# 128-column matmuls of the expert stages: issued in one or two bursts per expert pair, instead of at eleven places among the 64-column ones

## The chip, the cores and the metric

One core of a Trainium2 chip runs the whole program in one launch. The metric is the device time of that launch in microseconds (us). TensorE does the matmuls, VectorE (DVE) and ScalarE (ACT) empty its result banks, GpSimd (POOL) helps in the attention stages, and the SyncE queue (SP) issues the loads of the weights.

## What is computed

Two layers over 256 latent and 256 context tokens of width 1024. Each has a token mixer (windowed attention, then differential attention) and then a mixture of 32 SwiGLU experts, of which each token uses two. The last layer computes the latent tokens alone. What matters here is the mixture:

```python
def run(args):                       # one expert's tokens
    xblk, e = args
    u = xblk @ w_up[e]               # (tokens, 1024) @ (1024, 1024)
    return (silu(u[:, :512]) * u[:, 512:]) @ w_down[e]
yb = lax.map(run, (xb, blk_expert)).reshape(NB * MOE_BLOCK, D)
return zeros((T, D)).at[stok].add(yb[dest] * sw[:, None])
```

The router's choice of two experts for each token, and its weight `sw`, come just before. An expert has 1024x1024 weights up and 512x1024 weights down, all float32.

## The kernel before, in words

The function `moe` runs once for each layer. T is the number of tokens, 512 in layer 0 and 256 in layer 1. It takes the 32 experts as 16 **pairs**. An expert has room for 64 tokens, so a pair fills 128 rows: the first expert's matmuls write partitions 0 to 63 of a result bank, the second's write 64 to 127. Such a matmul has a 64-column weight operand (the tokens) and streams 512 columns of an expert's weights. This is what "64-column" means; the profile prints it as 128\*64, and one float32 matmul is two records. All others of the stage have 128 columns (128\*128).

One pair goes through these steps on TensorE, in this order:

- `up` (line 1195), for k = 0 to 7: four 64-column matmuls (8 records), which is one **step**. After it two loaded weight slots come free.
- `combine` (line 1276), after each of the eight steps: two 128-column matmuls of T columns that spread 128 output features of the previous pair back over the tokens. VectorE's `gated_add` (line 506) then adds the bank to the residual stream, 256 columns at a time.
- `gate` (lines 1202 to 1204): ScalarE and VectorE form the SwiGLU product from the two result banks of `up`.
- `gather` for the next pair, all 128-column: the routing weights' product (line 1174, emptied by the copies of lines 1177 and 1179), the first half of the token gather (line 1142), the transpose of the selection matrix (line 1158), then `turned` (line 1227), which transposes the gate's product, and the second half of the gather (line 1142).
- `down` (line 1239), four steps of 64-column matmuls. After the second and the third step `spread_tokens` (line 1184) transposes one half of the next pair's tokens, four 128-column transposes each time; VectorE adds the shift (line 1186). These are what the next pair's `up` reads.
- `weigh` (lines 1266 and 1267): ScalarE and VectorE scale the result and split it into two parts, which the next pair's `combine` reads.

In the last pair (`final`) `combine` starts only after step k = 3 (`HOLD` is 3), and three of the eight are done between the last `up` and the transposes of `gate_last`. In pair 0 there is nothing to combine. Pair 5 (`IF_AT`) has a branch after its `up` steps, for the case that an expert has more than 64 tokens.

Four things set the order. TensorE's order is that of the code (`manual_schedule(engines=PE)`). VectorE's and ScalarE's is chosen by a scheduler. The weights are loaded by one queue on SyncE, 24 loads of 512 KB a pair, each as soon as the slot that it writes has been read by TensorE. And the result banks are used in turn: `bank("G")`, `bank("C")`, `bank("B")` each rotate over two banks, and a matmul that starts on a bank waits until the engine that empties it is done.

```python
for k in range(KT):
    up(st, u, k)
    ...
    if prev and k >= HOLD * final:
        combine(l, T, prev, k - HOLD * final)
```

## Time and profile before

| | |
|---|---|
| runs | 1627.4, 1627.59, 1629.95 us; median 1627.59 us |
| profiled execution | span 1629.6 us from its first to its last instruction; only the run of 1629.95 us is as long, so 0.35 us lie around the span |
| TensorE busy | 1542.0 us, 95% |
| VectorE busy | 710.0 us, 44% |
| ScalarE busy | 383.5 us, 24% |
| loads from memory | 485.67 MB, mean 298 GB/s |

The time splits into stages: the modulation and attention of layer 0 until about 300 us, the experts of layer 0 until about 857 us, the attention of layer 1 until about 1105 us, the experts of layer 1 until about 1620 us, and the end. "Busy" of TensorE is an interval from an instruction's start to an end that the profile models, so 95% does not say that no time is lost between matmuls; the starts of the rows do.

### The profile page before, as it was taken

To read this page: it belongs to the slowest core of one execution; us is meant where nothing else is said; L and a number is where in the kernel's file an instruction comes from. 1 tells how busy PE (TensorE), PEld (TensorE's weight loads), DVE (VectorE), ACT (ScalarE), POOL (GpSimd) and SP (SyncE) were. 2 spreads that over 40 slices of the span, in tenths; PEclk is the share of its full clock that TensorE was granted. 3 is DMA by queue.
4 is the path that set the end of the run, shared out by engine and by line. 5 is a ranking of instruction groups with operands and counts; after the bars stand their busy time and mean duration, and the time that the engine had idled before them with its cause. 6 is when DMAs were issued, how large, how long until landed. Compare 5 with 4: busy or idle time off the path is not lost. (4 is left out here: it accounts for less than half of the span.)

```text
span 1629.6 us, 20216 instructions
## 1 busy us (share of the span) xinstructions
PE 1542.0 (95%) x7407; PEld 775.9 (48%) x7407; DVE 710.0 (44%) x1617; ACT 383.5 (24%) x823; POOL 185.2 (11%) x147
## 2 busy tenths in 40 slices
PE   6998999799999999999997889899999999999997
PEld 4765567443334444334435678673333333333334
DVE  3338852433333433333348977862232223232323
ACT  4426652101000111001114245651001100110112
POOL 2314541000000000000005373100000000000000
PEclk9999999899999999999997999998999999999999
DMA  9776236799989989999962842487999999999960
GB/s 315 236 232 225 90 104 225 298 362 366 377 323 360 377 349 363 375 374 375 362 200 88 294 166 103 170 294 298 405 402 351 397 401 402 398 394 400 403 241 27
DMA packets 169695, 485.67 MB, mean 298 GB/s; under 512 B 20825, under 2 KB 41586, under 8 KB 169586
## 3 DMA queue, kind: packets, MB, share of 16 engines
q1 hardware_dynamic: 169088, 483.66, 78.3%
q8 instruction: 63, 1.03, 0.3%
q10 hardware_dynamic: 498, 0.60, 0.1%
q14 instruction: 46, 0.38, 0.1%
HBM read 483.16 MB, written 1.05 MB: 297 GB/s over the span
## 5 line engine op out<-in xcount | busy, mean ns | idle before, releaser
L1195 PE MATMUL ps<-slotf,row 128*64 128x512 f32 x2048 | 492.4, 604 | 1.6 <-DVE row L1186 1.6
L506 DVE SCALAR_TENSOR_TENSOR slotf<-ps,mod,slotf 128x256 f32<-128x256 f32 x408 | 184.2, 481 | 382.5 <-PE ps L1276 349.8
L1195 PEld LDWEIGHTS ps<-slotf,row 128*64 128x64 f32 x2048 | 128.7, 136 | 228.2 <-issue 186.4
L1239 PE MATMUL ps<-slotf,row 128*64 128x512 f32 x960 | 225.8, 602 | 0.0
L543 PE MATMUL ps<-slotr,slotr 128*128 128x512 f32 x768 | 192.4, 403 | 11.1 <-DVE slotf L1395 5.7
L1276 PEld LDWEIGHTS ps<-row,row 128*128 128x128 f32 x512 | 76.3, 188 | 197.9 <-issue 177.2
L543 PEld LDWEIGHTS ps<-slotr,slotr 128*128 128x128 f32 x768 | 144.5, 193 | 48.9 <-DVE slotf L1395 6.1
L1276 PE MATMUL ps<-row,row 128*128 128x512 f32 (+1 forms) x512 | 156.4, 389 | 3.4 <-DVE slotf L506 3.3
L1202 ACT ACTIVATE row<-ps 128x512 f32<-128x512 f32 x30 | 17.9, 597 | 523.8 <-PE ps L1195 481.5
L1239 PEld LDWEIGHTS ps<-slotf,row 128*64 128x64 f32 x960 | 60.8, 136 | 112.6 <-issue 111.5
L1186 DVE TENSOR_TENSOR row<-ps,mod 128x512 f32<-128x512 f32 x64 | 44.2, 691 | 152.3 <-PE ps L1184 152.3
L1266 ACT ACTIVATE row<-ps,ty 128x512 fp32r<-128x512 f32 x60 | 41.2, 687 | 273.2 <-PE ps L1239 272.9
L518 POOL TENSOR_TENSOR slotr<-slotf,slotr 128x1024 fp32r<-128x1024 f32 x32 | 80.1, 2516 | 91.2 <-ACT slotr L514 78.9
L478 POOL TENSOR_TENSOR row<-row,row 128x512 f32<-128x512 f32 (+1 forms) x13 | 15.0, 1156 | 614.2 <-PE ps L1276 558.1
L1142 PE MATMUL ps<-slotr,row 128*128 128x512 f32 x256 | 70.9, 421 | 0.0
L1142 PE MATMUL ps<-slotf,row 128*128 128x512 f32 x128 | 66.3, 642 | 2.2 <-DVE s L1028 0.9
L1267 DVE SCALAR_TENSOR_TENSOR row<-ps,ty,row 128x512 fp32r<-128x512 f32 x60 | 45.0, 751 | 35.4 <-ACT row L1266 32.2
L514 ACT ACTIVATE slotr<-slotf 128x1024 fp32r<-128x1024 f32 x44 | 45.9, 1055 | 51.0 <-DMA slotf<-in_diff_w_qkv 23.8
L1142 PEld LDWEIGHTS ps<-slotr,row 128*128 128x128 f32 x256 | 48.1, 198 | 12.6 <-ACT row L1152 2.7
L1184 PEld LDWEIGHTS ps<-ident,row 128*128 128x128 f32 x256 | 27.0, 141 | 51.4 <-issue 50.3
L1494 DVE SCALAR_TENSOR_TENSOR row<-slotf,keep,row 128x512 f32<-128x512 f32 x42 | 49.2, 1184 | 1.1
L1358 PE MATMUL ps<-slotr,slotr 128*128 128x512 f32 x192 | 47.6, 399 | 0.0
(311 smaller groups left out, 1547.5 us busy)
## 6 DMA issues: line engine op xcount, KB each, us to landing
slotf<-in_moe_w_up SPq DMA_DIRECT2D x512, 512.0 KB, 6.7
slotf<-in_moe_w_down SPq DMA_DIRECT2D x256, 512.0 KB, 7.5
slotf<-in_mod_w SPq DMA_DIRECT2D x96, 512.0 KB, 6.2
slotf<-in_diff_w_qkv SPq DMA_DIRECT2D x24, 512.0 KB, 4.4
slotf<-in_win_w_qkv SPq DMA_DIRECT2D x12, 512.0 KB, 5.2
slotf<-in_win_w_o SPq DMA_DIRECT2D x8, 512.0 KB, 4.2
slotf<-in_diff_w_o SPq DMA_DIRECT2D x8, 512.0 KB, 3.8
slotf<-in_x SPq DMA_DIRECT2D x2, 512.0 KB, 4.2
```

The source lines that it names most:

```text
L506: ve.scalar_tensor_tensor(xT[k][:, sl], ps[:, sl], g[:, k, r:r + 1], xT[k][:, sl], op0=OP.mult, op1=OP.add)
L514: se.activation(hv, v, AF.Copy)
L518: (eng or (ge if split_i[0] % 3 == 0 else ve)).tensor_tensor(lv, v, hv.bitcast(F32), op=OP.subtract)
L543: pe.matmul(ps[t], h[:, x, ts], w[y][:, kk, :], start=(k + kk == 0 and n == 0), stop=(k + kk == KT - 1 and n == 2))
L1142: pe.matmul(g, P[:, t, :] if len(tok[t]) > 1 else P[:, t, :].bitcast(F32), v[:, hs], start=(t == 0 and i == 0), stop=(t == nt - 1 and i == ...
L1186: ve.tensor_tensor(o.rearrange("p (k c) -> p k c", k=4), ps.rearrange("p (k c) -> p k c", k=4), mods[l][:, 3, 4 * h:4 * h + 4, 0:1].to_bro ...
L1195: pe.matmul(u[h][64 * s:64 * s + 64, :], st["xt"][k // 4][:, c0:c0 + 64], w[s][1][:, h * 512:(h + 1) * 512], start=(k == 0), stop=(k == KT ...
L1239: pe.matmul(y[h][64 * s:64 * s + 64, :], acT[:, c0:c0 + 64], w[s][1][:, h * 512:(h + 1) * 512], start=(k == 0), stop=(k == 3))
L1267: ve.scalar_tensor_tensor(yl, y[h], wsl, yh.bitcast(F32), op0=OP.mult, op1=OP.subtract)
L1276: pe.matmul(ps[:, :T], part[:, ks], st["PT"][:, :T], start=(i == 0), stop=(i == 1))
L1358: pe.matmul(ps, w[x][:, k % 4, ms], oT0[k][1][:, y, :], start=(k == 0 and i == 0), stop=(k == KT - 1 and i == 2))
L1494: ve.scalar_tensor_tensor(acc, w[:, kk, :], keep[:, k + kk:k + kk + 1], acc, op0=OP.mult, op1=OP.add)
```

## The change

The table `HOLD` goes. Each pair's 128-column work moves to one or two places:

- Layer 0 (T = 512): the first four `combine` steps stand together after k = 3, behind the transposes of the second half of the tokens; the other four stand after k = 7, directly before `gather`.
- Layer 1 (T = 256): all eight stand after k = 7. Two of them share one result bank.
- The banks of `combine` are now C, C, B, B in turn. Before they were C alone.
- `spread_tokens` leaves `down`. In layer 0 the first half is transposed at the end of `gather` and the second half at k = 3 of the next pair. In layer 1 both halves are transposed at the end of `gather`, and the routing weights' product moves behind the second half of the gather.
- In the last pair `gate_last` calls the remaining `combine` steps in place of three of them.

```diff
--- before.py
+++ after.py
@@ -45,7 +45,6 @@
 MODS = range(0, 24, 3)
 LATE = (0,) * 4 + (4,) * 4 + (3,) * 4 + (1,) * 4 + (0,) * 8
 IF_AT = 5
-HOLD = 3
 BIG = 1e30
 RSQRT = float(0x5F3759DF)
 
@@ -1052,6 +1051,8 @@
 
         np_ = NE // 2
         prev = st = None
+        early_ks = range(0, KT // 2) if T == 512 else ()
+        late_ks = range(len(early_ks), KT)
         for p in range(np_):
             u = [bank("A"), bank("A")]
 
@@ -1062,15 +1063,18 @@
                     up(st, u, k)
                     if p == 0 and k == 1:
                         st["half"]()
-                    if p == 0 and k == 2:
-                        spread_tokens(l, st, 1)
-                        gather_weights(st["P"], WR, p, st, 2)
-                    if prev and k >= HOLD * final:
-                        combine(l, T, prev, k - HOLD * final)
+                    if k == KT // 2 - 1:
+                        if len(st["xt"]) < 2:
+                            spread_tokens(l, st, 1)
+                        if p == 0:
+                            gather_weights(st["P"], WR, p, st, 2)
+                        if prev:
+                            combine(l, T, prev, early_ks)
 
             if p == IF_AT:
                 with tc.manual_schedule(engines=PE):
                     ups()
+                    combine(l, T, prev, late_ks)
                 hs_ = [Slot() for _ in range(KT // 2)]
                 stream.ahead(len(free) - 1)
                 most = nc.values_load(cmi[0:1, 0:1], min_val=0, max_val=T)
@@ -1083,12 +1087,14 @@
                     st = gather(l, nt, 0, key, WR, tok, unit, weights, ri=post.ri)
                 if p != IF_AT:
                     ups()
+                rest = partial(combine, l, T, prev, late_ks) if prev and p != IF_AT else lambda: None
                 if final:
-                    acT = gate_last(u, [partial(combine, l, T, prev, k) for k in range(KT - HOLD, KT)])
+                    acT = gate_last(u, rest)
                 else:
                     ac = gate(u)
+                    rest()
                     nxt = gather(l, nt, p + 1, key, WR, tok, unit, None, lambda: turned(ac))
-                    y = down(nxt["acT"], partial(spread_tokens, l, nxt))
+                    y = down(nxt["acT"])
                     prev = {"parts": weigh(y, st["w"][:, 0:1]), "PT": st["PT"]}
                     st = nxt
         with tc.manual_schedule(engines=PE):
@@ -1098,7 +1104,7 @@
 
             def finals(c):
                 for k in (2 * c, 2 * c + 1):
-                    combine(l, T, {"parts": {k // 4: parts[c]}, "PT": st["PT"]}, k, k % 2)
+                    combine(l, T, {"parts": {k // 4: parts[c]}, "PT": st["PT"]}, (k,), k % 2)
                     last.append(after(k))
                     if len(last) > 2:
                         last.pop(0)()
@@ -1131,8 +1137,8 @@
                 for t in range(nt):
                     pe.matmul(wps[:, 0:1], P[:, t, :].bitcast(F32), ri[:, t:t + 1], start=(t == 0), stop=(t == nt - 1))
                 ve.tensor_copy(st["w"][:, 1:2], wps[:, 0:1])
-        else:
-            gather_weights(P, WR, p, st, 2 if unit else 3)
+        elif not unit:
+            gather_weights(P, WR, p, st, 3)
 
         def half(h):
             hs = slice(h * 512, (h + 1) * 512)
@@ -1165,6 +1171,10 @@
             st["half"] = partial(half, 1)
         else:
             half(1)
+            if unit:
+                gather_weights(P, WR, p, st, 2)
+            for h in range(1 + unit):
+                spread_tokens(l, st, h)
         return st
 
     def gather_weights(P, WR, p, st, n):
@@ -1204,7 +1214,7 @@
         ve.scalar_tensor_tensor(ac, ac, 0.5, u[1], op0=OP.mult, op1=OP.mult)
         return ac
 
-    def gate_last(u, between):
+    def gate_last(u, rest):
         th, ac, acT = row("s"), row("s"), row("x")
         halves = [slice(h * 256, (h + 1) * 256) for h in range(2)]
         for hs in halves:
@@ -1212,8 +1222,7 @@
         for hs in halves:
             ve.scalar_tensor_tensor(ac[:, hs], th[:, hs], 1.0, u[0][:, hs], op0=OP.add, op1=OP.mult)
             ve.scalar_tensor_tensor(ac[:, hs], ac[:, hs], 0.5, u[1][:, hs], op0=OP.mult, op1=OP.mult)
-        for f in between:
-            f()
+        rest()
         for h, hs in enumerate(halves):
             ps = bank("G")
             for k in range(2):
@@ -1229,7 +1238,7 @@
         se.activation(acT, ps, AF.Copy)
         return acT
 
-    def down(acT, spread=None):
+    def down(acT):
         y = [bank("B"), bank("B")]
         for k in range(4):
             w = [stream.next() for _ in range(2)]
@@ -1240,8 +1249,6 @@
                               w[s][1][:, h * 512:(h + 1) * 512], start=(k == 0), stop=(k == 3))
             for s in range(2):
                 w[s][0].free()
-            if spread and k in (1, 2):
-                spread(k - 1)
         return y
 
     def down_last(acT, c, wsl):
@@ -1268,13 +1275,21 @@
             parts.append((yh, yl))
         return parts
 
-    def combine(l, T, st, k, place=None):
-        ps = bank("C")
-        place = k % 4 if place is None else place
-        ks = slice(place * 128, (place + 1) * 128)
-        for i, part in enumerate(st["parts"][k // 4]):
-            pe.matmul(ps[:, :T], part[:, ks], st["PT"][:, :T], start=(i == 0), stop=(i == 1))
-        gated_add(l, 1, k, ps, T)
+    def combine(l, T, st, ks, place=None):
+        per = 512 // T
+        adds = []
+        for n, k in enumerate(ks):
+            if n % per == 0:
+                ps = bank("CCBB"[n // per % 4])
+            c = k % 4 if place is None else place
+            out = ps[:, (n % per) * T:(n % per + 1) * T]
+            for i, part in enumerate(st["parts"][k // 4]):
+                pe.matmul(out, part[:, c * 128:(c + 1) * 128], st["PT"][:, :T], start=(i == 0), stop=(i == 1))
+            adds.append((k, out))
+            if (n + 1) % per == 0 or n + 1 == len(ks):
+                for kk, v in adds:
+                    gated_add(l, 1, kk, v, T)
+                adds = []
 
     def overflow(l, nt, key, W, ri, tok, hT):
         T = nt * 128
```

Three places of the order of instructions show what moved. In `order` rows, `x4` means four alike in a row, and ps is a result bank.

TensorE in layer 0, pair 9, around the `up` step k = 3 (ps_5189, ps_5190 or ps_5182, ps_5183 are the two banks of `up`). Before, one step, its `combine`, and the next step:

```order
L1195 MATMUL ps_5189<-slotf_79,row_5159 64x512
L1195 MATMUL ps_5189<-slotf_55,row_5159 64x512
L1195 MATMUL ps_5190<-slotf_79,row_5159 64x512
L1195 MATMUL ps_5190<-slotf_55,row_5159 64x512
L1276 MATMUL ps_5232<-row_4927,row_5180 128x512
L1276 MATMUL ps_5232<-row_4927,row_5181 128x512
L1195 MATMUL ps_5189<-slotf_57,row_5172 64x512
```

The same place now:

```order
L1205 MATMUL ps_5183<-slotf_55,row_5145 64x512
L1194 MATMUL ps_5210<-ident,row_5138 128x128 x4
L1287 MATMUL ps_5217<-row_4927,row_5173 128x512
L1287 MATMUL ps_5217<-row_4927,row_5174 128x512
L1287 MATMUL ps_5222<-row_4927,row_5173 128x512
L1287 MATMUL ps_5222<-row_4927,row_5174 128x512
L1287 MATMUL ps_5227<-row_4927,row_5173 128x512
L1287 MATMUL ps_5227<-row_4927,row_5174 128x512
L1287 MATMUL ps_5232<-row_4927,row_5173 128x512
L1287 MATMUL ps_5232<-row_4927,row_5174 128x512
L1205 MATMUL ps_5182<-slotf_57,row_5215 64x512
```

One spread (line 1194) and four `combine` steps (line 1287) now stand in one run; between the other steps of `up` nothing is left.

VectorE in layer 0, at the end of a pair's `up`, from the gate's first multiplication (lines 1203 and 1213) to the drain of the gather's second half (lines 1150 and 1156). Before:

```order
L1203 SCALAR_TENSOR_TENSOR row_4896<-row_4895,ps_4803 128x512
L506 SCALAR_TENSOR_TENSOR slotf_133<-ps_4890,mod_236,slotf_133 128x256 x2
L1204 SCALAR_TENSOR_TENSOR row_4896<-row_4896,ps_4804 128x512
L1177 COPY ty_4902<-ps_4903 64x1 x2
L1179 COPY ty_4902<-ps_4903 128x1
L1150 TENSOR_SCALAR row_4945<-ps_4936,ty_4902 128x512
```

Now:

```order
L1213 SCALAR_TENSOR_TENSOR row_4876<-row_4875,ps_4796 128x512
L505 SCALAR_TENSOR_TENSOR slotf_135<-ps_4880,mod_236,slotf_135 128x256
L1214 SCALAR_TENSOR_TENSOR row_4876<-row_4876,ps_4797 128x512
L505 SCALAR_TENSOR_TENSOR slotf_135<-ps_4880,mod_236,slotf_135 128x256
L505 SCALAR_TENSOR_TENSOR slotf_135<-ps_4885,mod_236,slotf_135 128x256 x2
L505 SCALAR_TENSOR_TENSOR slotf_133<-ps_4890,mod_236,slotf_133 128x256 x2
L505 SCALAR_TENSOR_TENSOR slotf_133<-ps_4895,mod_236,slotf_133 128x256 x2
L1187 COPY ty_4902<-ps_4903 64x1 x2
L1189 COPY ty_4902<-ps_4903 128x1
L1156 TENSOR_SCALAR row_4945<-ps_4936,ty_4902 128x512
```

Eight adds now stand ahead of the copies of the routing weights (lines 1187 and 1189), where two stood.

TensorE in layer 1, from the gather's transposes to the first step of `down`. Before:

```order
L1227 MATMUL ps_10244<-ident,row_10222 128x128 x4
L1142 MATMUL ps_10251<-slotf_79,row_10226 128x512
L1142 MATMUL ps_10251<-slotf_55,row_10226 128x512
L1239 MATMUL ps_10256<-slotf_91,row_10249 64x512
L1239 MATMUL ps_10256<-slotf_81,row_10249 64x512
```

Now:

```order
L1236 MATMUL ps_10207<-ident,row_10162 128x128 x4
L1148 MATMUL ps_10214<-slotf_79,row_10194 128x512
L1148 MATMUL ps_10214<-slotf_55,row_10194 128x512
L1184 MATMUL ps_10219<-WR_8357,row_10194 128x2 x2
L1194 MATMUL ps_10224<-ident,row_10200 128x128 x4
L1194 MATMUL ps_10231<-ident,row_10217 128x128 x4
L1248 MATMUL ps_10238<-slotf_91,row_10212 64x512
```

The routing weights' product and both spreads now stand between the second half of the gather (line 1148) and `down` (line 1248); all four use the two banks of tag G in turn, so the first spread's bank is the one that the gather's second half was written to.

## Rows read from the trace of the kernel before

**Rows 1.** The page: the span, the engines' busy time, and the granted TensorE clock in 40 slices (tenths of full speed).

```profile
span 1629.6 us, 20216 instructions
PE 1542.0 (95%) x7407; PEld 775.9 (48%) x7407; DVE 710.0 (44%) x1617; ACT 383.5 (24%) x823; POOL 185.2 (11%) x147
...
PEclk9999999899999999999997999998999999999999
```

**Rows 2.** The chain that ended last: shares of the span by engine, and by line.

```profile
PE 20%; ACT 0%; DVE 0%; issue 0%; DVEq 0%; ACTq 0%
PE ps L1195 9%; PE ps L1239 4%; PE ps L1142 2%; PE ps L1276 2%; PE ps L1184 1%; PE ps L1253 0%; ACT row L1148 0%; PE ps L1174 0%; PE ps L491 0%; PE ps L1721 0%; DVEq L1768 0%; DVE slotf L506 0%; DVE row L1213 0%; ACT row L1211 0%; DVE row L1214 0%
```

**Rows 3.** Sums over stretches: one pair of layer 0, one gather in layer 0, one pair of layer 1, twelve us inside that pair, and the gather behind the branch of layer 0. The columns are the stretch, its length, busy time of PE, PEld, DVE, ACT and POOL with their counts, the granted clock, the DMA engines' busy share, and GB/s.

```profile
650.30:684.60 34.30, 34.30 (x156) 13.99 (x154) 12.90 (x27) 3.66 (x7) 0.00 (x0) 1.00 0.95 371
...
669.80:676.20 6.40, 6.40 (x38) 5.08 (x36) 2.48 (x7) 1.66 (x3) 0.00 (x0) 1.00 1.03 410
...
1428.60:1460.20 31.60, 31.51 (x140) 11.67 (x138) 9.22 (x18) 3.29 (x7) 0.00 (x0) 1.00 1.02 400
...
1436.00:1448.00 12.00, 12.00 (x56) 4.53 (x53) 3.55 (x8) 0.60 (x1) 0.00 (x0) 1.00 1.03 410
...
495.70:500.60 4.90, 4.82 (x16) 4.04 (x17) 1.75 (x5) 0.51 (x1) 0.00 (x0) 0.55 1.03 405
```

**Rows 4.** TensorE's timeline in layer 0: `down` with its spreads, some `up` and `combine` steps, and the next gather. The columns are start, length, engine, line, and the number of records; in brackets the idle time before and what ended it.

```profile
641.90 3.65 PE L1239 MATMUL ps<-slotf,row 128*64 128x512 f32 x16
645.49 0.66 PE L1184 MATMUL ps<-ident,row 128*128 128x128 f32 x4
...
647.94 0.66 PE L1184 MATMUL ps<-ident,row 128*128 128x128 f32 x4
...
652.11 0.73 PE L1276 MATMUL ps<-row,row 128*128 128x512 f32 x2
...
654.64 0.73 PE L1276 MATMUL ps<-row,row 128*128 128x512 f32 x2
...
669.83 0.73 PE L1276 MATMUL ps<-row,row 128*128 128x512 f32 x2
670.39 0.95 PE L1174 MATMUL ps<-WR,row 128*128 128x3 f32 x8
671.20 2.09 PE L1142 MATMUL ps<-slotr,row 128*128 128x512 f32 x8
673.13 0.60 PE L1158 MATMUL ps<-ident,row 128*128 128x128 f32 x4
673.57 0.60 PE L1227 MATMUL ps<-ident,row 128*128 128x128 f32 x4
```

**Rows 5.** TensorE's timeline in the last two pairs of layer 1; the columns as in Rows 4.

```profile
1578.42 3.65 PE L1239 MATMUL ps<-slotf,row 128*64 128x512 f32 x16
...
1586.81 7.04 PE L1195 MATMUL ps<-slotf,row 128*64 128x512 f32 x32
1593.78 0.50 PE L1276 MATMUL ps<-row,row 128*128 128x256 f32 x2
...
1596.08 0.50 PE L1276 MATMUL ps<-row,row 128*128 128x256 f32 x2
```

**Rows 6.** TensorE's timeline in the attention of layer 0: a run of eight 128-column matmuls of 256 columns, which follows 64-column ones; the columns as in Rows 4.

```profile
143.33 1.21 PE L757 MATMUL ps<-slotr,slotr 128*128 128x256 f32 x8
144.38 1.03 PE L782 MATMUL ps<-ident,row 128*128 128x128 f32 x8
```

**Rows 7.** The timeline of all engines in layer 0, behind the last `up` step of a pair; the columns as in Rows 4.

```profile
669.74 0.69 DVE L1203 SCALAR_TENSOR_TENSOR row<-row,ps 128x512 f32<-128x512 f32 x1 [0.80 <-ACT row L1202]
...
670.59 0.88 DVE L506 SCALAR_TENSOR_TENSOR slotf<-ps,mod,slotf 128x256 f32<-128x256 f32 x2 [0.16 <-PE ps L1276]
...
671.38 0.68 DVE L1204 SCALAR_TENSOR_TENSOR row<-row,ps 128x512 f32<-128x512 f32 x1
...
672.31 0.16 DVE L1179 COPY ty<-ps 128x1 f32<-128x1 f32 x1
...
673.38 0.69 ACT L1152 ACTIVATE row<-ps,ty 128x512 f32<-128x512 f32 x1 [3.67 <-PE ps L1142]
...
674.12 2.12 PE L1142 MATMUL ps<-slotr,row 128*128 128x512 f32 x8
...
676.17 3.65 PE L1239 MATMUL ps<-slotf,row 128*64 128x512 f32 x16
```

**Rows 8.** The timeline of all engines in layer 1: the second half of the gather, the start of `down`, and VectorE's drain of that half; the columns as in Rows 4.

```profile
1418.31 1.98 PE L1142 MATMUL ps<-slotf,row 128*128 128x512 f32 x4
...
1420.22 3.65 PE L1239 MATMUL ps<-slotf,row 128*64 128x512 f32 x16
1420.33 0.69 DVE L1146 COPY row<-ps 128x512 f32<-128x512 f32 x1 [3.58 <-PE ps L1142]
```

**Rows 9.** SyncE's load queue: its last loads of weights in the timeline; the columns as in Rows 4.

```profile
1557.50 10.95 SPq L178 DMA_DIRECT2D slotf<-in_moe_w_down  x8
```

**Rows 10.** The longest wait of SyncE's load queue: line, what it waited for, total us, times, the longest one.

```profile
SPq L178 <- PE ps L1195: 343.3, 223, 12.2
```

**Rows 11.** The timeline of all engines behind the branch of layer 0; the columns as in Rows 4.

```profile
495.78 1.46 PE L1174 MATMUL ps<-WR,row 128*128 128x3 f32 x8 [3.06 <-PEq L1077]
...
497.10 3.76 PE L1142 MATMUL ps<-slotr,row 128*128 128x512 f32 x8
```

## The prediction, made before the result was known

> **What bounds the kernel now.** I read the page first. TensorE is busy 95% of the span at a granted clock of nine tenths or more in all but three slices [rows 1], and the chain that ended last is TensorE's own: the expert stage's lines 1195, 1239, 1142, 1276 and 1184 lead it [rows 2]. So the time is that of TensorE's instruction stream. The sums over stretches say the same for a single pair: 34.3 of 34.3 us busy in layer 0, 31.5 of 31.6 in layer 1, at a clock of 1.00 [rows 3]. They also show what comes second: the loads run at 371 and 400 GB/s there, and 410 GB/s at most. A pair needs 24 loads of 512 KB; at 410 GB/s one takes 1.28 us and 24 take 30.7 us. That is a floor which layer 1 nearly touches.
>
> A busy engine can still lose time between instructions, so I then read the starts in TensorE's timeline. In the last pair of layer 1 four `up` steps stand without a `combine`: 6.97 us from the first start to the next 128-column matmul, 1.74 each, of which about 0.1 us in all belongs to that last change; so a clean step takes 1.72. With a `combine` behind each, the period is 2.30 [rows 5]. The two matmuls of 256 columns should add 0.24: in a run of eight, one takes (1.05 - 0.10) / 8 = 0.12 us, 0.10 being the entry from 64 columns [rows 6]. So going from 64 to 128 columns and back costs 2.30 - 1.72 - 0.24 = **0.34 us**, whatever work it carries. In layer 0 the period is 2.53 and the two matmuls of 512 columns are worth 0.23 each (eight gather matmuls take 1.93 with one slow entry): 2.53 - 1.72 - 0.46 = **0.35 us**. For a spread the period is 2.45, its four transposes are worth 0.44 (673.13 to 673.57): 2.45 - 1.72 - 0.44 = **0.29 us** [rows 4].
>
> **What the change removes.** It adds no matmul and takes none away; it takes away round trips.
> - Layer 0: in each of the pairs 1 to 14, seven `combine` steps stand alone (the eighth runs on into the gather); one burst at k = 3 remains. Six saved, 84 in all, and three in the last pair (four alone before, one burst now): 87 x 0.35 = 30.5 us.
> - Layer 1: seven saved in each of 14 pairs and four in the last: 102 x 0.34 = 34.7 us.
> - Spreads: two in each of 15 `down`s of each layer, 60 x 0.29 = 17.4 us. They now join runs that exist anyway.
>
> Together 82.6 us. The matmuls themselves keep their price in a run, by the rows just used.
>
> **What it adds.** Four waits, none of which the trace of before has; each is worked out from the order of instructions and the durations beside it.
> - *Layer 0, behind `up`.* Eight adds now stand on VectorE before the copies of the routing weights, which ScalarE's drain of the first gather half needs as its scale, and whose bank the transposes of the selection matrix need. Counted from the first `combine` behind `up` (669.83): the gate's first half ends at 0.60, the first add starts at 0.76, an add takes 0.40 (0.88 for two), so one add, the gate's second half and seven adds end at about 4.57, and the copies at 5.07 (before: 2.64) [rows 7]. TensorE has three more `combine` steps there, 6 x 0.23 = 1.38 us, so its first gather half ends at 3.30 + 1.38 = 4.68. The transposes wait for 5.12, 0.44 us. The second half starts at 4.29 + 1.38 = 5.67 without the wait; with it, at 5.12 + 0.88 = 6.0, and ScalarE's drain (5.1 + 0.69) allows that. The wait shrinks to **0.37 us** a pair, x 14 = 5.2 us. Bounds: nothing, if VectorE finishes by 4.7, and 1.1 us if its adds take 0.48 each (half of the 0.88 and a little more) and all of the delay shows.
> - *Layer 1, before the first spread.* Its bank is that of the gather's second half. VectorE drains that half from 0.11 after the point at which `down` starts now, for 0.69 [rows 8]; before, the spreads stood inside `down` and this was hidden. TensorE has only the routing weights' product (0.44 less the 0.10 of the change of width) to fill it: 0.80 + 0.05 + 0.05 to reload - 0.34 = **0.55 us**, x 15 = 8.3 us. Bounds: nothing, and 0.9 if the copy starts later.
> - *The branch pair*: VectorE has eight adds ahead of the branch, about 1 us later than before, and TensorE needs the next selection matrix from it: 2 us for two layers.
> - *The last pair*: `down`'s first bank (B) is now one that `combine` used, free only when VectorE has done six of eight adds: about 1 us, twice, 2 us.
>
> Sum of waits 17.5 us. What hides the rest: the early burst's adds (8 x 0.40 = 3.2 us) have the four `up` steps behind it (6.9 us); the tokens' shift at k = 3 (0.69) has the burst (1.84 us) as cover; `down`'s banks are free by 4.6 us, long before `down` starts at about 8.5.
>
> *Loads.* Layer 0's pair goes from 34.27 (641.90 to 676.17 [rows 4, 7]) to 34.27 - 6 x 0.35 - 2 x 0.29 + 0.37 = 31.96 us, still over the floor of 30.7. Layer 1's goes from 31.64 (1420.22 to 1578.42 is five pairs [rows 5, 8]) to 31.64 - 7 x 0.34 - 0.58 + 0.55 = 29.23, under it. But the queue runs far ahead: its last eight loads are issued from 1557.50 on, at the beginning of pair 14's `up`, so 38 loads are ahead of use [rows 9], some 49 us, and in the expert stages the queue waits for TensorE's slots, not the reverse [rows 10]. The deficit is 15 x 1.5 = 22 us. So loads cost nothing. Without that lead the floor would bind, as a rival below.
>
> **Sum.** 82.6 - 17.5 = 65 us. The profiled execution took 1629.95 us (span and 0.35 around it), which gives 1565; it is 2.4 us above the median, so **1562.5 us** for a median, 1562 rounded.
>
> **Rivals.**
> - *The new waits do not show.* The scheduler's margins could be kinder than my sums: 82.6 less the 4 us of branch and last pair gives 1549 us. For it: every wait is below 0.6 us. Against: the order shows the adds ahead of the copies. Chance 0.12.
> - *VectorE becomes the bound of the block behind `up`.* At 1.1 and 0.9 us a pair the waits are 15 + 14 + 4 = 33 us, the gain 50, the time 1578 us. Chance 0.10.
> - *Loads bind in layer 1.* If the lead is spent early, a pair takes 30.7 and layer 1 gains 0.9 x 15 = 14 us in place of 33: 1581 us. For it: 400 of 410 GB/s. Against: the 38 loads. Chance 0.06.
> - *The price is not that of the change of width* but of waits for a bank or a load, which move along: no change, about 1627 us. Against: the spacing is the same to 0.01 us at every step. Chance 0.02.
> - *TensorE's clock falls behind the longer bursts: slower than before.* [...] Against it: a gather with its eight transposes runs at 1.00 today [rows 3]. Chance 0.03. [...]
>
> **Numbers.** The forecast (gain of 55 to 75 us) has 0.67; with the others that makes 1. The range reaches from the case without waits (1549, less 3 for the rounding of the round trips) to those with full waits or bound loads (1578 and 1581, and 3 more): 1546 to 1584. It leaves out no change, the clock, and tails of the rest. About 0.2% is what a measurement can tell from no change here. Faster 0.95, within it 0.02, slower 0.03.
>
> **What would show it.** In the profile after: no `up` step with a period over 1.8 us except at k = 3 and 7; pairs of 32.0 and 29.2 us; about 0.4 us of TensorE idle before the selection matrix's transposes in layer 0 and 0.5 before the first spread in layer 1, both put down to VectorE; loads near 395 GB/s in layer 0 and 410 in layer 1, with no wait of TensorE for a load; the clock at 1.00. Wrong if clean steps take more than 1.75 us, if matmuls in a burst stand further apart than 0.23 or 0.12 us, or if the load waits appear before the last pairs.

## The result and the profile after

The changed kernel takes **1559.97 us** (median of 4 runs, 1558.15 to 1561.72); the kernel before, on the same chip, 1628.65 us (4 runs). The ratio is 0.9579, 95% interval 0.9565 to 0.9592: faster by 4.2%. The prediction said 1562 us, between 1546 and 1584.

The page of the changed kernel, whose lines answer to [rows 1] and [rows 2] (`up` is now line 1205, `down` 1248, the gather 1148, `combine` 1287, the spread 1194):

```profile
span 1557.9 us, 20210 instructions
...
PE 1459.4 (94%) x7407; PEld 802.0 (51%) x7407; DVE 692.2 (44%) x1617; ACT 385.2 (25%) x823; POOL 186.2 (12%) x147
...
PEclk9999999799999999999997999998999999999999
...
PE ps L1205 9%; PE ps L1248 5%; PE ps L1148 2%; PE ps L1287 2%; PE ps L1194 1%; PE ps L1260 0%; DVE row L1152 0%; ACT row L1154 0%; PE ps L490 0%; PE ps L1736 0%; DVEq L1783 0%; ACT row L1230 0%; DVE s L440 0%; DVE s L441 0%; PE ps L1236 0%
```

TensorE has the same 7407 matmul records as before and is busy 82.6 us less. A VectorE row, line 1152, is now in the chain: it is the drain of the gather's second half in layer 1, one of the new waits. The clock row is as before but for one slice (7 tenths in place of 8).

The sums over stretches, one pair of layer 0 and one of layer 1 (the columns as in [rows 3]):

```profile
616.00:648.00 32.00, 31.72 (x156) 15.14 (x154) 12.40 (x29) 3.76 (x6) 0.00 (x0) 1.00 1.00 395
1330.00:1359.00 29.00, 28.46 (x139) 12.09 (x138) 8.45 (x18) 3.34 (x6) 0.00 (x0) 1.00 1.03 409
```

The granted clock is 1.00 in both. Each stretch holds all transposes of a pair: 16 in layer 0, of which twelve stand close together, and 14 close together in layer 1. The loads run at 395 and 409 GB/s, as forecast. TensorE is no longer busy all the time: the 0.28 us of the first stretch and 0.45 of the 0.54 us of the second are the new waits (0.09 us stood in a pair of layer 1 before too, [rows 3]). Where they are, the timeline of layer 0 shows, `up` with its two bursts and the gather (the columns as in [rows 4]; it answers to [rows 4, 7]):

```profile
622.20 7.04 PE L1205 MATMUL ps<-slotf,row 128*64 128x512 f32 x32
...
629.17 0.66 PE L1194 MATMUL ps<-ident,row 128*128 128x128 f32 x4
629.58 2.09 PE L1287 MATMUL ps<-row,row 128*128 128x512 f32 x8
...
638.62 2.13 PE L1287 MATMUL ps<-row,row 128*128 128x512 f32 x8
...
640.38 2.83 DVE L505 SCALAR_TENSOR_TENSOR slotf<-ps,mod,slotf 128x256 f32<-128x256 f32 x7
...
643.46 0.16 DVE L1189 COPY ty<-ps 128x1 f32<-128x1 f32 x1
...
643.76 0.63 PE L1164 MATMUL ps<-ident,row 128*128 128x128 f32 x4 [0.28 <-DVE ty L1189]
...
644.58 2.10 PE L1148 MATMUL ps<-slotr,row 128*128 128x512 f32 x8
```

Four steps of `up` take 6.97 us, 622.20 to 629.17, the clean period of 1.74 with its change of width. Behind the last step the copies (line 1189) end late, behind the adds (line 505), and the transposes of the selection matrix wait 0.28 us for them. Counted from the burst's start (638.62) they begin at 5.14 us, and the second half of the gather at 5.96, where the prediction had 5.12 and 6.0. The same in layer 1 (answers to [rows 5, 8]):

```profile
1326.96 2.18 PE L1287 MATMUL ps<-row,row 128*128 128x256 f32 x16
...
1328.99 1.88 PE L1148 MATMUL ps<-slotf,row 128*128 128x512 f32 x4
...
1333.43 0.50 PE L1184 MATMUL ps<-WR,row 128*128 128x2 f32 x4
1333.63 0.69 DVE L1152 COPY row<-ps 128x512 f32<-128x512 f32 x1 [2.13 <-PE ps L1148]
...
1334.38 1.09 PE L1194 MATMUL ps<-ident,row 128*128 128x128 f32 x8 [0.45 <-DVE row L1152]
...
1335.40 7.09 PE L1248 MATMUL ps<-slotf,row 128*64 128x512 f32 x32
1342.32 10.04 PE L1205 MATMUL ps<-slotf,row 128*64 128x512 f32 x46
```

Sixteen `combine` matmuls take 2.03 us; the first spread waits 0.45 us for VectorE's drain, as the prediction describes it. The profile counts these 0.45 us from the modelled end of the routing weights' product. By the starts, the spread stands 0.95 us behind that product (1333.43 to 1334.38), and 0.36 us in e3_no_waits below, where it does not wait: the wait is 0.59 us. Summed over the trace the two waits read:

```profile
L1194 PE MATMUL ps<-ident,row 128*128 128x128 f32 x256 | 38.3, 282 | 6.9 <-DVE row L1152 6.7 <-ACT row L1154 0.3
...
L1164 PE MATMUL ps<-ident,row 128*128 128x128 f32 x96 | 17.5, 295 | 3.7 <-DVE ty L1189 3.7
```

(busy time, mean ns of one, idle time before them and what ended it): 6.7 us in layer 1 (15 pairs) and 3.7 us in layer 0 (13 pairs), 10.4 us of idle time in all, where the prediction had 13.5 us of waits.

From the first start of `up` in one pair to that in the next, in us, read from TensorE's starts in both traces and in those of the experiments:

| | layer 0, pair | layer 0, pair 5 (branch) | layer 1, pair 0 | layer 1, pair | layer 1, pair 5 (branch) |
|---|---|---|---|---|---|
| before | 34.27 | 40.77 | 32.07 | 31.64 | 36.00 |
| after | 31.77 | 37.58 | 32.62 | 29.19 | 35.56 |
| predicted | 31.96 | | | 29.23 | |
| e1_spreads_back | 32.40 | 38.24 | 30.99 | 29.12 | 35.70 |
| e2_combine_back | 34.01 | 41.22 | 31.05 | 31.60 | 36.20 |
| e5_four_bursts | 31.77 | 37.18 | 32.48 | 30.21 | 34.44 |
| e3_no_waits | 31.47 | 36.17 | 30.61 | 28.73 | 36.02 |
| e4_one_burst | 33.91 | 42.26 | 31.05 | 29.18 | 35.57 |
| e7_branch_early | 31.47 | 37.49 | 30.61 | 28.73 | 33.86 |
| e8_narrow_combine | 34.97 | 39.62 | 31.96 | 30.77 | 35.27 |
| e9_f32_combine | 37.42 | 41.25 | 32.04 | 33.21 | 37.57 |

Of the span's 71.7 us, the experts of layer 0 give 38.2 and those of layer 1 33.8 (from the first start of `up` to the end of the last `combine`). The code outside is untouched: the start is 3.9 us shorter, the attention of layer 1 4.5 us longer, the end 0.3 shorter. The start is not the change's doing: e8, whose code up to there is that of before, starts its first `up` at 299.5 us, 4.0 earlier than before's profile. The attention of layer 1 may be in part: it takes 250.8 us before and 251.1 to 252.7 us in e8, e9 and e2, which have no bursts in layer 0, but 254.5 to 256.1 us in the change and in every edit that has one. Why is left open.

### The profile page after: what moved, and what is told of

Read it like the earlier page. It is cut to its first block, busy times and chain, and to the rows that moved or that the text cites. A ratio compares the mean times of both kernels' runs of the same rounds, so it can differ in the third digit from the quotient of the medians.

```text
span 1557.9 us, 20210 instructions
## 1 busy us (share of the span) xinstructions
PE 1459.4 (94%) x7407; PEld 802.0 (51%) x7407; DVE 692.2 (44%) x1617; ACT 385.2 (25%) x823; POOL 186.2 (12%) x147
## 5 line engine op out<-in xcount | busy, mean ns | idle before, releaser
L1205 PE MATMUL ps<-slotf,row 128*64 128x512 f32 x2048 | 450.8, 595 | 2.1 <-DVE row L1196 2.1
L1205 PEld LDWEIGHTS ps<-slotf,row 128*64 128x64 f32 x2048 | 145.6, 137 | 291.1 <-issue 275.3
L1248 PE MATMUL ps<-slotf,row 128*64 128x512 f32 x960 | 212.6, 595 | 0.0
L505 DVE SCALAR_TENSOR_TENSOR slotf<-ps,mod,slotf 128x256 f32<-128x256 f32 x408 | 167.3, 476 | 62.4 <-PE ps L1287 29.7
L1248 PEld LDWEIGHTS ps<-slotf,row 128*64 128x64 f32 x960 | 66.2, 137 | 124.9 <-issue 118.1
L1213 DVE SCALAR_TENSOR_TENSOR row<-row,ps 128x512 f32<-128x512 f32 x30 | 20.6, 688 | 234.4 <-ACT row L1212 234.4
L1287 PE MATMUL ps<-row,row 128*128 128x512 f32 (+1 forms) x512 | 104.5, 349 | 1.1 <-DVE slotf L505 1.0
```

The source lines that it names most:

```text
L505: ve.scalar_tensor_tensor(xT[k][:, sl], ps[:, sl], g[:, k, r:r + 1], xT[k][:, sl], op0=OP.mult, op1=OP.add)
L1205: pe.matmul(u[h][64 * s:64 * s + 64, :], st["xt"][k // 4][:, c0:c0 + 64], w[s][1][:, h * 512:(h + 1) * 512], start=(k == 0), stop=(k == KT ...
L1248: pe.matmul(y[h][64 * s:64 * s + 64, :], acT[:, c0:c0 + 64], w[s][1][:, h * 512:(h + 1) * 512], start=(k == 0), stop=(k == 3))
L1287: pe.matmul(out, part[:, c * 128:(c + 1) * 128], st["PT"][:, :T], start=(i == 0), stop=(i == 1))
```

## Experiments

All edits are to the changed kernel unless said otherwise. The kernel before took 1627.5 to 1628.9 us beside these runs.

### The spreads back among the steps of `down`: e1_spreads_back

```diff
-            for h in range(1 + unit):
-                spread_tokens(l, st, h)
...
-                    y = down(nxt["acT"])
+                    y = down(nxt["acT"], partial(spread_tokens, l, nxt))
...
+            if spread and k in (1, 2):
+                spread(k - 1)
```

> The change with one part undone: the two spreads of a pair stand inside down again, the combine bursts stay. Theory (each run of 128-column work among 64-column steps costs a fixed price, 0.29 us for a spread): 60 x 0.29 = 17.4 us dearer than the change (1560.0), less the 0.45 us of wait before the first spread of layer 1, which goes in 15 pairs (6.8 us): 1570.6 us. Rival, banks (the gain is that combine has four result banks and VectorE adds in a row, not the width): the spreads cost nothing where they stand, 1553 us (the wait goes). Rival, loads (the load queue sets the pace of layer 1): layer 1 unchanged, only layer 0 pays 30 x 0.29: 1569 us.

Measured: **1566.91 us** (1566.83 to 1568.76), ratio 0.9626 (0.9611 to 0.9640), 3.7 us under my number. A pair of layer 0 is 0.63 us longer: two round trips of 0.29 and a little. But a pair of layer 1 is 0.07 us *shorter*: two round trips (0.58 us) come back, and the wait for line 1152 (0.59 us by the starts, where I had 0.45) goes. So the term for the spreads stands, and in layer 1 the new wait eats it whole. Another 1.6 us is pair 0 of layer 1 (30.99 in place of 32.62), which has its reason in the clock (0.69 in its first two steps in the change, 1.00 in e1); e3_no_waits shows it.

### `combine` back after every step: e2_combine_back

```diff
-                        if prev:
-                            combine(l, T, prev, early_ks)
+                    if prev and k >= 3 * final:
+                        combine(l, T, prev, (k - 3 * final,))
...
-                    combine(l, T, prev, late_ks)
...
-                rest = partial(combine, l, T, prev, late_ks) if prev and p != IF_AT else lambda: None
+                rest = (lambda: [combine(l, T, prev, (k,)) for k in range(KT - 3, KT)]) if final else lambda: None
```

> The change with the other part undone: combine after each up step as before, in the C banks alone; the spreads stay where the change put them. Theory: of the gain only the spreads' 17.4 us are left, less 6.8 us of wait in layer 1: 1628.7 - 17.4 + 6.8 = 1618 us, with combine periods of 2.53 and 2.30 us again. Rival, banks: all of the gain gone, and the spreads worth nothing: 1628 to 1635 us. Rival, loads: layer 0 as the theory (spreads 8.7 us), layer 1 at the pace of before: 1620 us.

Measured: **1624.38 us** (1620.98 to 1626.74, 9 runs), ratio 0.9971 (0.9960 to 0.9982). The gain all but goes, so it came from the bursts. The periods of `up` with a `combine` are 2.53 and 2.30 us again, but I missed by 6 us. Some 2 us of that are layer 1's wait, which is 0.59 and not 0.45 us: its pair is 31.60 in place of 31.64, so there the spreads gain nothing. TensorE's timeline in layer 0 at k = 3 shows the rest:

```profile
586.25 0.66 PE L1193 MATMUL ps<-ident,row 128*128 128x128 f32 x4
586.66 0.71 PE L1286 MATMUL ps<-row,row 128*128 128x512 f32 x2
587.68 1.94 PE L1204 MATMUL ps<-slotf,row 128*64 128x512 f32 x8 [0.32 <-DVE row L1195]
```

The next `up` step needs the spread's tokens with VectorE's shift (line 1195, 0.69 us). One `combine`, 0.46 us, does not cover that; a burst of four, 2.02 us in the change (629.58 to 631.60), does. It costs 14 x 0.32 = 4.5 us, and the early burst is worth that much as cover, beside its round trips.

### Layer 1 in four bursts: e5_four_bursts

```diff
-        late_ks = range(len(early_ks), KT)
+        late_ks = range(len(early_ks), KT) if T == 512 else (6, 7)
...
+                    if T == 256 and prev and k in (1, 3, 5):
+                        combine(l, T, prev, (k - 1, k))
```

> The change, but in layer 1 the eight combine steps stand in four bursts of two (after k = 1, 3, 5, 7), each burst sharing one bank of tag C; no work added or taken away, layer 0 untouched. Theory: three round trips more in 15 pairs, 45 x 0.34 = 15.3 us: 1575 us, pairs of layer 1 of 30.2 us instead of 29.19. Rival, banks: combine is back in the C banks alone with VectorE's adds between, layer 1 loses its 35 us: about 1595 us. Rival, loads: layer 1's pairs stay where the load queue puts them: 1560 us.

Measured: **1571.51 us** (1570.49 to 1572.16), ratio 0.9649 (0.9634 to 0.9664). A pair of layer 1 goes from 29.19 to 30.21 us: 1.02 us for three more round trips, 0.34 each, the price that the rows of before gave. The numbers of matmuls and of adds are the same. The total is 3.5 us under my number; 2.1 of it are the branch pair, which became 1.1 us shorter and not 1.0 longer.

### The two waits taken away: e3_no_waits

In layer 0 the routing weights' product goes ahead of the late burst, so that VectorE copies it before the adds; in layer 1 it takes a bank of tag C, so that the first spread does not meet the bank of the gather's second half.

```diff
-                    rest()
-                    nxt = gather(l, nt, p + 1, key, WR, tok, unit, None, lambda: turned(ac))
+                    nxt = gather(l, nt, p + 1, key, WR, tok, unit, None, lambda: turned(ac), mid=rest)
...
         elif not unit:
             gather_weights(P, WR, p, st, 3)
+        if mid:
+            mid()
...
-                gather_weights(P, WR, p, st, 2)
+                gather_weights(P, WR, p, st, 2, "C")
```

> The change with its two new waits taken away: in layer 0 the routing weights' product stands ahead of the late burst, so that its copies stand ahead of the adds on VectorE; in layer 1 that product goes to a bank of tag C, so that the first spread does not need the bank of the gather's second half. Theory: 14 x 0.29 + 15 x 0.45 = 10.9 us less than the change: 1549 us, pairs of 31.5 and 28.74 us. Rival, loads: layer 1 is already at the pace of the loads, only layer 0 gains: 1556 us. Rival, waits come back elsewhere on VectorE: 1560 us.

Measured: **1546.99 us** (1546.28 to 1549.39), ratio 0.9506 (0.9493 to 0.9519): faster than both kernels. Pairs lose 0.30 and 0.46 us, the idle times above, and no wait stands before the first spread any more:

```profile
1323.30 0.50 PE L1185 MATMUL ps<-WR,row 128*128 128x2 f32 x4
...
1323.66 1.24 PE L1195 MATMUL ps<-ident,row 128*128 128x128 f32 x8
...
1324.83 7.09 PE L1249 MATMUL ps<-slotf,row 128*64 128x512 f32 x32
```

(The eight transposes take 1.17 us here and 1.02 in the change: the second four read what VectorE drains, and start at 1324.25 us, just behind the end of line 1153 at 1324.19. So 0.59 us of wait goes and some of it comes back.)

Pair 5 of layer 0 and pair 0 of layer 1 lose 1.4 and 2.0 us as well, pair 5 of layer 1 is 0.5 us longer; the sum is the 13 us. But these three pairs differ for the most part by TensorE's clock. The first two steps of `up` in layer 1, in the change and in e3 (the columns as in [rows 3]):

```profile
1069.85:1075.00 5.15, 5.15 (x16) 1.42 (x16) 0.00 (x0) 0.00 (x0) 0.00 (x0) 0.69 0.12 26
...
1063.98:1067.56 3.58, 3.58 (x16) 1.05 (x16) 0.00 (x0) 0.00 (x0) 0.00 (x0) 1.00 0.17 56
```

The same 16 records take 5.15 us at a granted clock of 0.69 and 3.58 at 1.00, so 1.57 of the 2.0 us are the clock. Behind the branch of layer 0 the gather takes 9.26 us in the change and 7.87 in e3, at 0.63 and 0.78, which is the 1.4 us; in layer 1 it is 7.92 and 8.26 at 0.78 and 0.69. No part of this edit was meant to do that, and e1, e2 and e4 have 1.00 in those two steps too. So about 10.8 of the 13 us (13 x 0.30 and 15 x 0.46) are the two waits, and the other 2 are the clock's. Layer 1's pair is 28.73 us to pair 14, 2 us under the floor of its loads, 30.7 us for 24 of them at 410 GB/s [rows 3].

### The price by itself, at the same width and the other: e8_narrow_combine, e9_f32_combine

Both are edits of the kernel *before*, and differ in width alone: `combine` stands after every step, as one unsplit float32 product in place of a high and a low part (but for the end of a layer, which keeps the two parts). In e9 it is 128 columns wide, in e8 two tiles of 64 columns, like `up`.

```diff
-            yh, yl = row("e", dt=F32R), row("e", dt=F32R)
+            yh = row("e")
...
-            ve.scalar_tensor_tensor(yl, y[h], wsl, yh.bitcast(F32), op0=OP.mult, op1=OP.subtract)
-            parts.append((yh, yl))
+            parts.append((yh,))
...
+        for s in range(2 if len(parts) == 1 else 0):         # e8
+            c0 = place * 128 + 64 * s
+            pe.matmul(ps[64 * s:64 * s + 64, :T], parts[0][:, c0:c0 + 64], st["PT"][:, :T].bitcast(F32), start=True, stop=True)
...
+        if len(parts) == 1:                                  # e9
+            pe.matmul(ps[:, :T], parts[0][:, ks], st["PT"][:, :T].bitcast(F32), start=True, stop=True)
```

> The kernel before, with the combine steps at their eleven places, but each as 64-column matmuls: two column tiles like those of up, unsplit float32 in place of a high and a low part (VectorE's second half of weigh goes too). A tile pair takes 0.86 us for 512 columns and 0.43 for 256, by the up rows, where the two 128-column matmuls took 0.46 and 0.24. My theory (the price is the change of width, 128 columns against 64): without a change of width no round trip is paid at these places; the period of a step is 1.72 + 0.86 = 2.58 us in layer 0 (2.53 before) and 1.72 + 0.43 = 2.15 in layer 1 (2.30 before); pairs of 35.0 and 30.8 us; total about 1627 us (1620 to 1633). Rival, any interruption of the up steps costs 0.34 us whatever its width: steps of 2.93 and 2.50 us, total about 1700 us.

> The kernel before, with the combine steps where they were and 128 columns wide, but with one unsplit float32 matmul (two records) in place of two fp32r matmuls of a high and a low part; VectorE's second half of weigh goes. My theory (width): periods of 2.53 and 2.30 us as before, total 1628.6 us (within 2). Rival, the price comes from the change of data type between float32 and fp32r, not of width: steps of 2.18 and 1.96 us, total about 1558 us.

Measured: e8 **1625.02 us** (1623.48 to 1626.70, 10 runs), ratio 0.9981 (0.9971 to 0.9990); e9 **1695.02 us** (1690.72 to 1697.18), ratio 1.0407 (1.0388 to 1.0426). TensorE's timeline of e8, in layer 0 and in layer 1:

```profile
368.90 1.89 PE L1195 MATMUL ps<-slotf,row 128*64 128x512 f32 x8
370.62 1.03 PE L1279 MATMUL ps<-row,row 128*64 128x512 f32 x4
371.48 1.89 PE L1195 MATMUL ps<-slotf,row 128*64 128x512 f32 x8
...
1178.76 1.89 PE L1195 MATMUL ps<-slotf,row 128*64 128x512 f32 x8
1180.48 0.60 PE L1279 MATMUL ps<-row,row 128*64 128x256 f32 x4
1180.91 1.89 PE L1195 MATMUL ps<-slotf,row 128*64 128x512 f32 x8
```

and of e9:

```profile
372.40 1.94 PE L1195 MATMUL ps<-slotf,row 128*64 128x512 f32 x8
374.27 1.12 PE L1278 MATMUL ps<-row,row 128*128 128x512 f32 x2
375.32 1.08 PE L1195 MATMUL ps<-slotf,row 128*64 128x512 f32 x4
...
1215.61 1.94 PE L1195 MATMUL ps<-slotf,row 128*64 128x512 f32 x8
1217.48 0.70 PE L1278 MATMUL ps<-row,row 128*128 128x256 f32 x2
1218.11 1.94 PE L1195 MATMUL ps<-slotf,row 128*64 128x512 f32 x8
```

In e8 the periods are 2.58 and 2.15 us and the steps of `up` and `combine` follow each other at 1.72 and 0.86 (0.43): nothing is paid for the interruption. In e9 they are 2.92 and 2.50. Between the two lies the change of width alone: over a pair's `up`, from the first to the last start (19.32 against 21.76 us in layer 0, 16.33 against 18.77 in layer 1), seven round trips cost 2.44 us, 0.35 each, in both layers. Where the work is done does not matter; its width does. My number for e9 was wrong by 66 us, for another reason: I took an unsplit float32 product of 128 columns for no dearer than the two fp32r ones. Its two records take the 0.86 (0.43) us of e8 in place of 0.46 (0.24), which is 8 x 0.40 = 3.2 and 8 x 0.19 = 1.5 us a pair, measured 3.15 and 1.57. (Such records of 512 columns stand 0.43 us apart in a run, too: four in the gather of the changed kernel take from 1328.99 to 1330.70.) The rival, the data type as the price, is refuted: e9 has one type and pays. Its `up` steps pay what those of before do, less the 0.40 and 0.19: 2.92 - 0.40 = 2.52 and 2.50 - 0.19 = 2.31, against 2.53 and 2.30.

### Layer 0 in one burst too: e4_one_burst

```diff
-        early_ks = range(0, KT // 2) if T == 512 else ()
+        early_ks = ()
```

> The change, with all eight combine steps of layer 0 in one burst behind k = 7 too; at k = 3 the spread of the second half stands alone. My theory (round trips pay, but the adds of VectorE, 0.80 us for a combine of 512 columns against 0.46 on TensorE, and its 0.69 us shift need something on TensorE to lie beside): the burst waits for banks that the adds free, the copies of the routing weights end about 8.3 us behind the burst's start, the selection matrix's transposes wait some 1.4 us more than now, and the spread at k = 3 loses its cover, about 0.5 us: a layer 0 pair goes from 31.77 to about 33.6 us, 14 pairs, total 1585 us (1578 to 1592), with waits for DVE L505 or L1189 on TensorE. Rival, the number of round trips alone sets the time: one run with the spread at k = 3 as before, only 0.06 us a pair less, total 1559 us.

Measured: **1594.70 us** (1593.34 to 1596.44), ratio 0.9794 (0.9779 to 0.9809): 34.7 us dearer than the change, with no round trip more. I expected 25; a pair is 2.14 us longer, not 1.8, and the branch pair 4.7. At k = 3 the step behind the spread, which now has no cover, waits 0.78 us (line 1196), where I had 0.5; the branch pair I had taken for one like the others. The timeline behind the last `up` step of a layer 0 pair:

```profile
381.55 2.11 PE L1287 MATMUL ps<-row,row 128*128 128x512 f32 x8
...
383.31 5.96 DVE L505 SCALAR_TENSOR_TENSOR slotf<-ps,mod,slotf 128x256 f32<-128x256 f32 x15
383.94 3.05 PE L1287 MATMUL ps<-row,row 128*128 128x512 f32 x8 [0.28 <-DVE slotf L505]
...
389.82 0.63 PE L1164 MATMUL ps<-ident,row 128*128 128x128 f32 x4
```

The second half of the burst takes 3.05 us, not 2.1, since its banks come free one add pair (0.80 us) at a time, and the transposes of line 1164 start 8.27 us behind the burst's start, as worked out (5.14 in the change). So VectorE is what limits how much may stand in one place, and two bursts in layer 0 are right for its 512 columns.

### The branch pair: e7_branch_early

An edit of e3_no_waits: the `combine` steps that stand ahead of the branch move to behind k = 5.

```diff
+                    if p == IF_AT and k == KT // 2 + 1:
+                        combine(l, T, prev, late_ks)
...
                     ups()
-                    combine(l, T, prev, late_ks)
```

> e3_no_waits (1547.0 us), where in the pair with the branch (pair 5 of each layer) the combine steps that stand ahead of the branch move to behind k = 5. My theory: after the change the branch comes late because VectorE still has these adds to do (from the burst's start to their end 4.0 us), while TensorE has nothing; with the adds beside the up steps the pair saves 4.0 us less the burst (2.03 and 1.84 us) and one round trip (0.35), so 1.7 and 1.8 us in the two layers: 1543.5 us, and idle time of TensorE before the gather of about 3 us in place of 4.8. Rival, the wait behind the branch is not due to the adds but to the branch itself: one more round trip in each layer, 1547.7 us.

Measured: **1547.65 us** (1544.33 to 1550.78), ratio 0.9512 (0.9499 to 0.9525): no different from e3. By pairs I was right in layer 1 (36.02 to 33.86 us) and wrong in layer 0 (36.17 to 37.49). TensorE's first work behind the branch, in layer 0 and in layer 1:

```profile
477.05 1.15 PE L1186 MATMUL ps<-WR,row 128*128 128x3 f32 x8 [3.40 <-PEq L1082]
...
1229.07 3.48 PE L1150 MATMUL ps<-slotf,row 128*128 128x512 f32 x4 [3.21 <-PEq L1082]
```

With the adds out of the way, 3.2 to 3.4 us without work remain: the branch itself. So the adds were the cause only of what is above that: in e3 these waits are 2.88 and 4.84 us, so nothing in layer 0 and 1.6 us in layer 1. From the start of the last `up` record to the gather, the burst included, it is 5.51 us in e3 and 3.99 in e7 in layer 0, 1.5 saved; 7.53 and 3.81 in layer 1, 3.7 saved; and the burst among the steps costs 2.2 in each. In layer 1 the gather is 0.7 us shorter besides (7.58 against 8.26 us to the start of `down`), at a granted clock of 0.80 in place of 0.69. In layer 0 it is 0.65 us longer (8.52 against 7.87, at 0.80 and 0.78): that is one stop of 0.66 us among the transposes of line 1166, for which the profile shows no wait; its cause is left open.

### A shorter lead of the loads: e6_short_lead

```diff
+        held = [Slot() for _ in range(28)] if l else []
...
-            for s in itertools.chain(*h_slots):
+            for s in itertools.chain(*h_slots, held):
                 s.free()
```

> The change, with 28 weight slots held back during layer 1's experts, so that the loads run 10 ahead of use there in place of 38. My theory (the lead of 38 loads is what lets a pair take 29.19 us where its 24 loads need 30.7): 28 loads of 1.28 us, 36 us, of lead are missing; the deficit of 15 pairs, 1.5 us each, is 22 us and only 10 loads, 13 us, cover it, less what bursts of use need at once; from some pair on a pair takes 30.7 us, layer 1 gains 10 to 15 us less and the total is about 1572 us (1566 to 1580), with TensorE waiting for DMA in the later pairs. Rival, the lead plays no part (a load is quicker than 1.28 us when it has to be, or the slots come free in time anyway): 1560 us and pairs of 29.19 us to the end.

Measured: **1611.49 us** (1610.23 to 1613.44), ratio 0.9906 (0.9889 to 0.9922): 51.5 us dearer than the change, not 12. From the page of this kernel, the chain by line and the loads of `up` (how many, KB each, median us from issue to landing):

```profile
DMA slotf<-in_moe_w_up 7%; PE ps L1249 4%; PE ps L1206 3%; PE ps L1149 2%; PE ps L1288 1%; PE ps L1195 1%; PE ps L1261 0%; DVE row L1153 0%; ACT row L1155 0%; PE ps L490 0%; PE ps L1737 0%; DVEq L1784 0%; ACT row L1231 0%; DVE s L441 0%; DVE s L440 0%
...
slotf<-in_moe_w_up SPq DMA_DIRECT2D x512, 512.0 KB, 8.0
```

and sums over some seven pairs of layer 1, then over `up` and over `down` of pair 8 (the columns as in [rows 3]), and the queue's wait for `down` in that pair (total us, times, the longest one):

```profile
1330.00:1560.00 230.00, 221.62 (x986) 91.60 (x987) 62.38 (x131) 23.34 (x42) 0.00 (x0) 1.00 0.99 389
...
1338.00:1355.00 17.00, 16.21 (x66) 4.96 (x63) 1.50 (x2) 1.15 (x2) 0.00 (x0) 1.00 1.02 409
...
1364.00:1371.00 7.00, 7.00 (x37) 2.55 (x37) 1.37 (x3) 0.23 (x1) 0.00 (x0) 1.00 0.82 304
...
SPq L177 <- PE ps L1249: 9.8, 4, 7.2
```

Loads now lead the chain, and layer 1's pairs take 31.7 to 33.9 us (40.1 with the branch): more than the floor of 30.7. The lead matters, then, and the rival is refuted. My size was off because I counted the average alone. The loads do run at 409 GB/s during `up` and the gather. But by the end of the burst the ten slots are all in use again, and none comes free until the first step of `down` is done: in pair 8 the queue issues a load at 1358.03 us and the next at 1366.43, and a load takes about 8 us from issue to landing (8.0, the median of the last row of the page). So the engines have too little to do during `down`, 304 GB/s over 7 us, and the average over seven pairs is 389. By an estimate from these rows, `down` loses 7.0 x (1 - 304/409) = 1.8 us; pair 8 takes 33.0 us, 3.8 more than the change's 29.19, of which 1.5 are the floor and 1.8 this gap. What the other 0.5 us are, and whether it is the same in every pair, is left open.

## Why the prediction was right, point by point

- **The round trip** (0.34, 0.35): right. Its size comes back as 0.34 where three are added (e5), as 0.35 where width alone changes: e9, whose `combine` is 128 columns wide, pays 0.35 us a visit, and e8, whose two tiles have the 64 columns of `up`, pays nothing (2.58 = 1.72 + 0.86 us). What TensorE does in the 0.35 us, no run here shows.
- **The spread's round trip** (0.29): right; `down` went from 8.39 to 6.92 us, 2 x (0.29 + 0.44) = 1.46, and e1 gives 0.63 us back in layer 0. In layer 1 the new wait was as large as the two round trips.
- **Layer 0's wait** (0.37): 0.28 to 0.30 (trace, e3). Its mechanism, adds ahead of the copies, is shown by e3, which takes it away. The pair is 31.77 us in place of 31.96; the other 0.1 us is not put down to one place.
- **Layer 1's wait** (0.55): right, 0.59 by the starts; 0.45 as the profile counts idle time, and 0.46 come back in e3. The two 0.05 us in its sum stand in no row of before, and the sum as written makes 0.56; in the change the spread starts 0.06 us behind the drain's end (1334.32 to 1334.38).
- **The branch pair** (1 us in each layer, 2 in all): the sum came out by luck, the parts did not. TensorE's idle time before the gather behind the branch went from 3.06 [rows 11] to 2.86 us in layer 0, where there is no new wait, and from 2.74 to 4.72 in layer 1. e7 shows that in layer 1 the eight adds ahead of the branch are 1.6 us of it. So the pair saved 3.19 us in layer 0, more than the others there, and 0.44 in layer 1, two less than the others. Layer 1 before and after:

```profile
1287.21 0.58 PE L1174 MATMUL ps<-WR,row 128*128 128x2 f32 x4 [2.74 <-PEq L1077]
...
1239.93 3.38 PE L1148 MATMUL ps<-slotf,row 128*128 128x512 f32 x4 [4.72 <-PEq L1081]
```

- **The last pair** (about 1 us, twice): the wait came as described. In layer 1 `down` starts at 1535.10, behind VectorE's sixth add, which ends at 1535.00 (the profile names a row of ScalarE that ended 0.7 us before); the idle time there is 1.24 us in place of 0.32, and 1.28 in place of 0.32 in layer 0. But the prediction says that the trace of before has none of its waits, and does not count that the last pair of before has two of its own, in which `combine` waits for VectorE's adds to free a bank of tag C: 0.44 and 0.55 us in layer 1, 0.60 and 0.74 in layer 0. With four banks they go. From the start of `up` to that of this `down` (the function `down_last`) the pair saved 1.98 us in layer 1 and 1.50 in layer 0, where the terms make 0.36 and 0.05. Layer 1 before and after:

```profile
1604.15 0.50 PE L1276 MATMUL ps<-row,row 128*128 128x256 f32 x2 [0.44 <-DVE slotf L506]
...
1535.10 3.67 PE L1260 MATMUL ps<-slotf,row 128*64 128x256 f32 x32 [1.24 <-ACT row L1230]
```

- **Not foreseen**: pair 0 of layer 1 has no `combine`, so the spread at k = 3 has only the routing weights' product to cover VectorE's shift. The step behind it waits half a microsecond for that, in the changed kernel's timeline of TensorE, and the pair became 0.55 us longer than before. The early burst of layer 0 is such a cover (e2, e4), which the prediction named without saying what it is worth.

```profile
1082.01 4.51 PE L1205 MATMUL ps<-slotf,row 128*64 128x512 f32 x20 [0.51 <-DVE row L1196]
```

- **Loads**: right that they cost nothing. The lead is being spent: the last eight loads are issued from 1506.46 us on, 18 us into pair 14, with 24 loads ahead of use in place of 38 [rows 9]. Those 14 loads, 18 us, are near the predicted deficit of 22. e6 shows that the lead was needed.
- **The clock**: 1.00 in stretches with the bursts and with 16 and 14 transposes among the other matmuls, so the rival in which it falls behind them is refuted. It still falls behind the branch and at the start of layer 1's experts, as it did before: 0.55 over 4.9 us behind the branch of layer 0 before [rows 3] and 0.63 over the 9.26 us of that gather after, where eight gather matmuls take 3.56 us at 0.50 (480.51 to 484.07) against 1.93 in a pair at 1.00 [rows 3, 4]; and 0.69 in layer 1's first two steps, before and after.
- **The sum**: 65 us were forecast, and the medians differ by 68.7 (the two profiled executions by 71.7). Layer 0's experts gave 38.2 us against the 32.0 of its terms: 2.5 of that are the pairs' 0.19 us, 1.5 the branch pair, 1.5 the last pair and 0.8 pair 0. Layer 1's gave 33.8 against 33.1, and that it is so near is luck in part: 1.6 us more in the last pair stand against 1.0 and 0.6 less in the branch pair and in pair 0. The rival without waits (1549 us) is what e3 then made, 1547, but some 2 us of what e3 saves are the clock's.

## What to carry to other kernels

Before grouping work on TensorE, take the period of a step with and without the interruption from one trace and subtract the inserted work at the rate that it has in a run: what remains is the price of an entry (0.34 and 0.35 us here), and it can be multiplied. Then list what each moved matmul leaves behind on the engine that empties its bank: a group may hold as much as that engine can add up before the next dependent step (in e4, at 0.80 us for a pair of adds, the burst's second half took 3.05 us in place of 2.1), and the first dependent one needs other work between as cover (in e2 it waited 0.32 us for a shift of 0.69 us behind 0.46 us of work). When the time falls below a floor of the loads, look at how many loads are ahead of use, how long one takes to land and for how long no slot comes free (in e6 10 loads, 8.0 us and 8.4 us), not at the average rate alone. And before two runs are compared by their totals, compare the granted clock of the same stretch in both (0.69 and 1.00 for the change and e3 here, 1.57 us over 16 records).

## What the runs showed of the hardware

- The change between 64 and 128 columns costs 0.34 to 0.35 us for a visit of two matmul records (before, e9) or four (e5), whether they stream 256 or 512 columns and whether they are fp32r (before, e5) or float32 (e9). Two 64-column tiles among 64-column steps cost nothing beyond their own time (e8: 2.58 us for 1.72 + 0.86, and 2.15 for 1.72 + 0.43).
- An unsplit float32 product of 128 columns takes nearly twice the time of a high and a low fp32r part for 512 columns, 0.86 against 0.46 us (e9: 3.15 us more over eight; 0.43 us a record in a run of the change), and is as slow as two tiles of 64 columns (e8: 0.86).
- The same 512 KB loads ran at 409 GB/s with 24 or more ahead of use (the change). With 10 ahead (e6) they ran at 409 during `up`, at 304 during `down`, behind a stretch of 8.4 us without an issue, and at 389 over 230 us of layer 1.
- The same two steps of `up` took 5.15 us at a granted clock of 0.69 (the change) and 3.58 at 1.00 (e3), though the code ahead of them is the same but for layer 0's experts.
